# A two-block transformer step on one core: decays one projection chunk later, a modulation slab moved, units in strict turn, a shorter routing chain

## The chip, the cores and the metric

The kernel runs on one core of one Trainium2 chip. The metric is device time in microseconds (us) of one execution, lower is better; times of several executions are given by their median. The engines are named as in the profile: PE (matrix products; PEld its weight loads), DVE (vector), ACT (activation functions), POOL (GpSimd), SP (it only issues transfers here). The 16 DMA engines move all data.

## What is computed

Two transformer blocks, one after the other, on 256 tokens of width 1024, all in 32-bit floats. Cut to what matters:

```python
# first block
h = rmsnorm(x); proj = h @ w_mix_in            # 3592 columns
y_sc  = sc_b * conv(sc_c * sc_h)
g     = -exp(a_log) * softplus(ga + dt_bias)   # decays of the gated delta rule
beta  = sigmoid(gb)
o     = gated_delta_rule_chunked(q, k, v, g, beta)
y_sb  = stick_breaking_attention(sq, sk, sv)
x = x + concat(y_sc, o * silu(gz), y_sb) @ w_mix_out
x = x + (silu(gate) * val) @ w_ffn_down        # gate, val = conv(rmsnorm(x) @ w_ffn_up)
x = rmsnorm(x)
# second block
mod = silu(c) @ w_ada + b_ada                  # six modulation vectors of 1024
h = rms_norm(x) * (1 + sc1) + sh1
x = x + gt1 * rms_norm(attention(h) @ w_out)
h2 = rms_norm(x) * (1 + sc2) + sh2
logits = h2 @ w_router + b_router              # 32 experts, the 4 largest of each token
x = x + gt2 * rms_norm(sum over the 4 experts of gate * expert(h2))
```

## The kernel before

**Weights.** Nearly all the traffic is weights, and SP issues their loads in one fixed order. The dense part reads 67 slabs of 1 MB and 24 slabs of the modulation matrix `w_ada` (1 MB each) into six half slots of pool A. The experts' part reads 32 x 6 slabs of 2 MB (`in_we`, loaded in `load_m`, line 246) into ten slots. `TURNS = "FABADACCEG"` names the pool of each of the ten; slab m goes to the pool of m mod 10, and when the products have read a slab, `free_m` issues the load of the slab ten places on into the slot that came free. The first twelve slabs are those of two fixed experts, so their loads need no routing; the rest are read by numbers that the router gives. The pools are stacked in memory: pools C and G are opened after the dense part has closed its stack `sx`, at the same addresses. C (two slots of 16 KB a partition) lies where the dense part's unit buffers were, G where its normalised tokens were. E's slot holds `hT`, the tokens for the router's logits, until the logits are done.

**Units.** For exactness a dense slab is split into halves ("units"), each a rounded high part (ACT, or POOL; line 407) and the remainder (DVE, or POOL every n-th; line 412). Four buffers of 8 KB hold the units; PE multiplies three times a pair (lines 451, 485 to 487). `unit()` splits up to four units ahead.

**First block.** `weave` (line 124) records several generators in one order: `delta()` (the gated delta rule), `queries()`, `sticks()` (stick-breaking), `silus()`, `projections()` (the filler: 24 matrix products of 256 columns a projection, in chunks of 9, 9 and 6) and `filler()` (two `w_ada` slabs). Each step yields estimates of engine time, and those alone decide who is recorded next; on the chip each engine then works through its own queue in that order. In `delta()` the decays `g` and `beta` come from a few tiny DVE operations (lines 760 to 764); after them PE forms cumulative sums with products of 4 columns (767 to 776), DVE copies them out (`gcol` 771, `grows` 779), PE spreads `grows` over the partitions (785), and from that follow `dec`, `kb`, the products 812, and five levels of 844. `sticks()` goes from products 938/939 over ACT, DVE and POOL to products 962.

**Between the blocks' halves.** After the output projection come a norm and a transposition (line 358) for each of two token halves. While DVE and ACT work on the second half, PE multiplies slabs of `w_ada` with `ada(0)` (line 501, four products of 512 columns a slab): 2 in `filler`, `F0` = 4 between the two transpositions, 1 behind the second, the eighth and the final transposition in passes 0 and 1 of the feed-forward.

```python
            flipped(xn[:, 0, :], 0, take_scaled(lambda kc: col("w_norm_ffn", kc)))
            for _ in range(F0):
                next(fill)
            pool_los["of"] = 1
            split_ahead(1)
            flipped(xn[:, 1, :], 1, take_scaled(lambda kc: col("w_norm_ffn", kc)))
            split_ahead(2)
            pool_los["of"] = 0
            for _ in range(7 - F0 - F00):
                next(fill)
```

Then 11 passes of the feed-forward (`up` twice, `down` twice a pass), the attention of the second block with another `weave`, its output projection (the last `LAST` = 2 units in `last_products`), the routing, and the experts in the order of `ORDER`.

**Routing.** `turned` transposes x, `logits` multiplies it with the router's weights, DVE finds the four largest of each token (`sel`), PE counts places (lines 1579 to 1585), `select` makes a selection matrix `S` (1697), `gather` multiplies it with x (1710), ACT copies the result out (1712), `turn` transposes it (1721), and the first expert's products (1752) begin. `keep_warm` issues products that compute nothing.

Of the kernel before, what the change touches and what calls it, by code (L numbers as in the profile page):

```python
# [11 lines left out]
F32R = mybir.dt.float32r  # L12
BF = mybir.dt.bfloat16
I32 = mybir.dt.int32
AF = mybir.ActivationFunctionType
OP = mybir.AluOpType
# [5 lines left out]
P = 128  # L22
# [6 lines left out]
UW = 1024  # L29
# [7 lines left out]

PLACES = "531240531240531240530125304530412530412530412530412504153045230512340512340521435012345"

TURNS = "FABADACCEG"  # L40
NS = len(TURNS)
F00 = 2
F0 = 4
F1 = 3
LAST = 2

WARM = (4, 6, 9, 1, 2, 9, 12, 20)
# [114 lines left out]
def fl(t):  # L162
    return t.rearrange("p a b -> p (a b)")
# [3 lines left out]
def kernel(ctx: ExitStack, tc: tile.TileContext, x_in, cols_in, rows_in, const_in, cona_in, conb_in, rpb_in,  # L167
                      ws_in, wf_in, we_in, b1_in, b2_in, out, dbg=None):
    nc = tc.nc
# [11 lines left out]

    x = pers.tile([P, 2, D], F32, name="x")
    sx = ctx.enter_context(ExitStack())
    parts = sx.enter_context(tc.tile_pool(name="parts", bufs=4))
    xnp = sx.enter_context(tc.tile_pool(name="xnp", bufs=1))
    hp = sx.enter_context(tc.tile_pool(name="hp", bufs=1))
    cols = hp.tile([P, NKEPT], F32, name="cols")
# [62 lines left out]
    def load_all(names):  # L250
        for m in range(NS):
            if TURNS[m] in names:
                load_m(m)
# [38 lines left out]
    def con(name):  # L292
        a, b = CONST[name]
        return cst[:, a:b]
# [3 lines left out]
    def bank(pool=None):  # L298
        return (pool or ps).tile([P, 512], F32, name="mm")

    def keep_warm(n):

        b = bank()
        for _ in range(n):
            nc.tensor.matmul(b, warm[:, 0:1].to_broadcast([P, P]), warm[:, 0:1].to_broadcast([P, 512]), start=True, stop=True)  # L305

    def rsqrt(r, v, n):

        rsqrt_start(r, v)
        rsqrt_end(r, v, n)  # L310

    def rsqrt_start(r, v):
        nc.scalar.activation(r, v, AF.Ln)  # L313
        nc.scalar.activation(r, r, AF.Exp, scale=-0.5)

    def rsqrt_end(r, v, n):
        a = small.tile([P, 4], F32, name="nwt")
        nc.vector.tensor_mul(a[:, :n], v, r)
        nc.vector.scalar_tensor_tensor(a[:, :n], a[:, :n], -0.5, r, op0=OP.mult, op1=OP.mult)
        nc.vector.scalar_tensor_tensor(r, a[:, :n], 1.5, r, op0=OP.add, op1=OP.mult)  # L320
# [64 lines left out]
    with sx:  # L385
# [11 lines left out]
        def split(u, hi_on=None):  # L397

            s, h = divmod(u, 2)
            s = WS_DENSE[s]  # L400
            raw = s_slab[s][:, h * UW:(h + 1) * UW]
            t = parts.tile([P, 2, UW], F32R, name="u")
            hi, lo = t[:, 0, :], t[:, 1, :]
            if hi_on:
                hi_on.tensor_copy(hi, raw)
            else:
                nc.scalar.activation(hi, raw, AF.Copy)  # L407
            pool_los["n"] += 1
            on_pool = pool_los["of"] and pool_los["n"] % pool_los["of"] == 0
            loads.extend([("A", 0.95), ("G", 2.3) if on_pool else ("V", 1.13)])  # L410
            eng = nc.gpsimd if on_pool else nc.vector
            eng.tensor_tensor(lo, raw, hi, op=OP.subtract)  # L412
            hi_lo[u] = (hi, lo)
            if h == 1:
                slab_read(s)
# [103 lines left out]
        with ExitStack() as s1:  # L519
# [205 lines left out]
            def delta():  # L725
# [36 lines left out]
                    nc.vector.scalar_tensor_tensor(g[:, c, :], ga[:, c, :], -1.0, ea, op0=OP.mult, op1=OP.mult)  # L762
                nc.vector.tensor_scalar(beta, beta, 1.0, None, op0=OP.add)
                nc.vector.reciprocal(beta, beta)
                yield [("v", 1.1)]
                gcp = bank(pg)
                nc.tensor.matmul(gcp[:, 0:4], con("uincl"), g[:, 0, :], start=True, stop=True)
                nc.tensor.matmul(gcp[:, 4:8], ones, g[:, 0, :], start=True, stop=False)
# [231 lines left out]
        with ExitStack() as s2:  # L1000
# [32 lines left out]
            flipped(xn[:, 1, :], 1, take_scaled(lambda kc: col("w_norm_ffn", kc)))  # L1033
            split_ahead(2)
            pool_los["of"] = 0
            for _ in range(7 - F0 - F00):
                next(fill)
            dump("x1", x)
            sf = s2.enter_context(ExitStack())
# [1 line left out]
            with ExitStack() as s3:  # L1041
# [60 lines left out]
                for i in range(NFF // 2):  # L1102
                    up(2 * i)
                    next(biases, None)
                    if i < 2:
                        next(fill)
                    up(2 * i + 1)
                    if i:
                        next(biases, None)
                    if 0 < i < NFF // 2 - 1:  # L1110
                        for j in (2 * i - 2, 2 * i - 1):
                            down(j, (0, 1), *unit())
                    if 2 <= i < 2 + len(WX):
                        n = len(WS) + i - 2
                        s_slab[n] = fx.tile([P, SW], F32, name="w")
                        nc.sync.dma_start(s_slab[n], ws_in[n])
                    if i == 1:
                        for _ in fill:
                            pass
                    if i == 7:  # L1120
                        fill = ada(1)
                    if i >= 7:
                        next(fill)
# [359 lines left out]
            def turned(c, h):  # L1483
                b = bank()
                for k in range(4):
                    nc.tensor.transpose(b[:, k * P:(k + 1) * P], x[:, c, h * 512 + k * P:h * 512 + (k + 1) * P], ident)
                return b
# [14 lines left out]
            b = turned(0, 1)  # L1502
            x_sums(1, 0)
            nc.scalar.activation(fl(hT[:, 1]), b, AF.Copy)
            bs = [turned(1, 0)]
            x_sums(0, 1)
            x_sums(1, 1)
            keep_warm(WARM[4])
            logits(0, 1)
            bs.append(turned(1, 1))  # L1510
            nc.vector.tensor_copy(fl(hT[:, 2]), bs[0])
            v = row_means(ssx)
            rsqrt_start(rx, v)
            nc.scalar.activation(fl(hT[:, 3]), bs[1], AF.Copy)
            rsqrt_end(rx, v, 2)
            for h in range(2):
                logits(1, h)
            dump("x4", x)
            keep_warm(WARM[5])


    for k in "CG":
        pools[k] = ctx.enter_context(tc.tile_pool(name="slabs" + k, bufs=TURNS.count(k), reuse_waits="tile"))
    ek2 = ctx.enter_context(tc.tile_pool(name="ek2", bufs=2, side="right", reuse_waits="tile"))
    psa = ctx.enter_context(tc.tile_pool(name="psm", bufs=1, space=PSUM, reuse_waits="tile"))
# [21 lines left out]
        w.ek = stack.enter_context(tc.tile_pool(name="ek", bufs=2, reuse_waits="tile"))  # L1547
        return w

    load_all("CEG")  # L1550
    s6 = ctx.enter_context(ExitStack())
    w = open_work(s6)

# [25 lines left out]
    nc.tensor.matmul(b[:, 0:NE], con("uincl"), sel[:, 0, :], start=True, stop=True)  # L1579
    nc.tensor.matmul(b[:, NE:2 * NE], ones, sel[:, 0, :], start=True, stop=False)  # L1580
    nc.tensor.matmul(b[:, NE:2 * NE], con("uincl"), sel[:, 1, :], start=False, stop=True)
    nc.tensor.matmul(b[0:NE, 64:96], ones[:, 0:NE], sel[:, 0, :], start=True, stop=False)
    nc.tensor.matmul(b[0:NE, 64:96], ones[:, 0:NE], sel[:, 1, :], start=False, stop=True)
    nc.tensor.matmul(b[0:NE, 96:97], sel[:, 0, :], one_c, start=True, stop=False)
    nc.tensor.matmul(b[0:NE, 96:97], sel[:, 1, :], one_c, start=False, stop=True)
    nc.vector.tensor_tensor(place, b[:, 0:64].rearrange("p (c e) -> p c e", c=2), sel, op=OP.mult)
    cnt = rt.tile([NE, NE + 1], F32, name="cnt")
    nc.scalar.activation(cnt, b[0:NE, 64:97], AF.Copy)
    dump("cnt", cnt)
# [109 lines left out]
                nc.vector.tensor_scalar(slotted(G, c, tb), slot_numbers(tb), pc, gt(c), op0=OP.is_equal, op1=OP.mult)  # L1699
        return tb, S, G  # L1700

    def gather(w, tb, S, G):

        R = P // tb
        n = D // R
        xg = w.ek.tile([P, 512], F32, name="xg")
        b = bank()
        for c in range(2):
            for p in range(R):
                nc.tensor.matmul(b[p * tb:(p + 1) * tb, 0:n], S[:, c, p * tb:(p + 1) * tb],  # L1710
                                 x[:, c, p * n:(p + 1) * n], start=(c == 0), stop=(c == 1))
        nc.scalar.activation(xg[:, 0:n], b[:, 0:n], AF.Copy)
        return R, tb, xg, G

    def turn(w, R, tb, xg, G):
# [112 lines left out]
    def selects(pos):  # L1828
        rank = ORDER[pos]
        pos_, gate_ = by_rank(rank)  # L1830
        return [select(w, first, tb, pos_, gate_ if pos else None) for first, tb in cut(CAPS[rank])]

    blks = [gather(w, *a) for a in selects(0)]
    blks = [turn(w, *a) for a in blks]
    gates()
    chosen = selects(1)
# [301 lines left out]
```

## Time and profile before

| | |
|---|---|
| median of 3 runs | 1470.18 us (1468.39 to 1471.1) |
| the profiled execution's own time | 1470.03 us |
| its span, first to last instruction | 1468.3 us |
| PE busy / DVE / ACT / POOL | 93% / 37% / 31% / 4% |
| bytes moved | 506.66 MB, mean 345 GB/s |
| mean granted PE clock | 0.981 of full |

The profiled execution lies 1.7 us above its span and 0.15 us below the median, so what the rows say is read as if it stood at the median. A busy PE means that matrix products are in flight, not that they run at full rate; PE's granted clock is given as a share, 1.00 for 2.4 GHz and 0.50 for 1.2 GHz. Busy shares are means over stages that have different limits; the time of an edit is read from its own stage.

### The profile page before, as it was taken

What the parts mean: (1) busy time and instruction counts of PE and PEld (TensorE: products, weight loads), DVE (VectorE), ACT (ScalarE), POOL (GpSimd) and SP (SyncE); (2) the same over time, 40 slices, a digit from 0 to 9 for tenths busy, and PEclk for the clock granted to TensorE, in tenths of its full rate; (3) what the DMA queues carried; (4) which work ended last, traced back from release to release, by engine and by line L of the source; (5) the groups of instructions that cost most, each with busy time, mean ns of one, the idle gap of its engine ahead of it and who ended that gap; (6) DMA issues with size and microseconds to landing.
All of it is one profiled execution on the core that took longest, in us unless ns stands there. A gap on an engine that the chain in (4) does not pass through costs nothing.

```text
span 1468.3 us, 21778 instructions
## 1 busy us (share of the span) xinstructions
PE 1358.5 (93%) x8879; PEld 728.9 (50%) x8879; DVE 547.3 (37%) x1259; ACT 453.7 (31%) x972; POOL 55.7 (4%) x32
## 2 busy tenths in 40 slices
PE   8999999999999999999889889899998799899884
PEld 6899789998688753233233223233332233233221
DVE  6754677766757852121121121121211112121112
ACT  6454565554657541111111111111111111111111
POOL 3222010000000000000000000000000000000000
PEclk9999999999999999999999999999999999999997
DMA  7422586656746699999999999999999999999993
GB/s 319 144 87 87 198 327 235 266 212 230 240 172 232 256 384 427 427 428 427 427 428 428 428 428 427 427 427 427 427 427 428 428 427 427 428 427 427 428 428 159
DMA packets 43433, 506.66 MB, mean 345 GB/s; under 512 B 5024, under 2 KB 5280, under 8 KB 6880
## 3 DMA queue, kind: packets, MB, share of 16 engines
q1 hardware_dynamic: 42752, 503.61, 83.3%
q8 instruction: 72, 1.18, 0.3%
q10 hardware_dynamic: 576, 1.61, 0.3%
q14 instruction: 33, 0.27, 0.1%
HBM read 504.14 MB, written 1.05 MB: 344 GB/s over the span
## 4 chain that ended last, share of the span: by engine, by line
PE 56%; DMA 37%; ACT 3%; DVE 3%; issue 1%; SPq 0%; DVEq 0%; ACTq 0%
DMA w<-in_we 37%; PE mm L451 16%; PE mm L1752 13%; PE mm L1795 5%; PE acc L485 3%; PE acc L486 3%; PE acc L487 3%; PE acc L1820 2%; PE mm L1710 2%; PE mm L1790 1%; PE mm L844 1%; PE mm L501 1%; PE acc L1274 1%; PE mm L305 0%; ACT u L407 0%
## 5 line engine op out<-in xcount | busy, mean ns | idle before, releaser
L1752 PE MATMUL mm<-w,xT 128*64 128x512 f32 (+1 forms) x2432 | 434.5, 617 | 52.6 <-DMA w<-in_we 51.7
L1752 PEld LDWEIGHTS mm<-w,xT 128*64 128x64 f32 (+1 forms) x2432 | 129.9, 127 | 341.3 <-issue 257.4
L1761 DVE TENSOR_SCALAR h<-mm 128x256 f32<-128x256 f32 x58 | 24.6, 424 | 685.9 <-PE mm L1757 685.9
L451 PE MATMUL mm<-hT,u 128*128 128x256 f32 x2064 | 265.4, 288 | 0.0
L451 PEld LDWEIGHTS mm<-hT,u 128*128 128x128 f32 x2064 | 254.8, 194 | 13.9 <-issue 10.6
L1762 ACT ACTIVATE a<-h 128x256 f32<-128x256 f32 x58 | 24.2, 417 | 484.3 <-DVE h L1761 484.3
L412 DVE TENSOR_TENSOR u<-w,u 128x1024 fp32r<-128x1024 f32 x115 | 144.6, 1261 | 67.8 <-ACT u L407 64.9
L407 ACT ACTIVATE u<-w 128x1024 fp32r<-128x1024 f32 x133 | 139.0, 1054 | 30.5 <-PE acc L487 23.8
L1795 PE MATMUL mm<-w,aT 128*64 128x512 f32 x640 | 141.9, 595 | 5.5 <-ACT aT L1773 5.4
L1795 PEld LDWEIGHTS mm<-w,aT 128*64 128x64 f32 x640 | 44.3, 137 | 90.2 <-issue 80.0
L1800 ACT ACTIVATE y<-mm 128x512 f32<-128x512 f32 x38 | 22.7, 597 | 208.8 <-PE mm L1795 138.7
L1790 PE MATMUL mm<-w,aT 128*32 128x512 f32 x576 | 65.9, 596 | 10.4 <-ACT aT L1773 9.6
L1710 PE MATMUL mm<-x,S 128*32 128x256 f32 (+1 forms) x448 | 57.7, 465 | 3.5 <-DVE S L1697 3.5
L412 POOL TENSOR_TENSOR u<-w,u 128x1024 fp32r<-128x1024 f32 x19 | 45.8, 2409 | 319.3 <-PE mm L305 203.0
L1083 DVE SCALAR_TENSOR_TENSOR fcv<-mm,cols,fcv 128x255 f32<-128x255 f32 x88 | 42.3, 481 | 24.9 <-ACT fcv L1080 23.4
L1728 ACT ACTIVATE xT<-mm,mod,gs 128x64 f32<-128x64 f32 (+1 forms) x152 | 46.6, 386 | 5.8 <-PE mm L1721 5.2
L1730 DVE TENSOR_SCALAR xT<-mm,gs,mod 128x64 f32<-128x64 f32 (+1 forms) x152 | 38.7, 319 | 14.4 <-PE mm L1721 14.4
L1790 PEld LDWEIGHTS mm<-w,aT 128*32 128x32 f32 x576 | 16.7, 109 | 47.7 <-issue 31.1
L1710 PEld LDWEIGHTS mm<-x,S 128*32 128x32 f32 (+1 forms) x448 | 18.7, 119 | 40.4 <-issue 31.6
L1080 ACT ACTIVATE fcv<-mm,cols 128x256 f32<-128x256 f32 x44 | 20.8, 472 | 55.4 <-PE mm L451 55.4
L1962 POOL TENSOR_TENSOR fs<-fs,x 128x512 f32<-128x512 f32 x1 | 1.3, 1262 | 929.7 <-ACT fr L313 929.7
L485 PE MATMUL acc<-u,gh 128*128 128x512 f32 x88 | 34.9, 397 | 0.0
(555 smaller groups left out, 1368.2 us busy)
## 6 DMA issues: line engine op xcount, KB each, us to landing
w<-in_we SPq DMA_DIRECT2D x192, 2048.0 KB, 34.9
w<-in_ws SPq DMA_DIRECT2D x90, 1024.0 KB, 4.9
nb<-in_rpb SPq DMA_DIRECT2D x4, 512.0 KB, 7.8
w<-in_ws SPq DMA_DIRECT2D x2, 512.0 KB, 6.9
bt<-in_b SPq DMA_DIRECT2D x3, 256.0 KB, 9.8
out<-fs SPq DMA_DIRECT2D x3, 256.0 KB, 2.1
x<-in_x SPq DMA_DIRECT2D x1, 512.0 KB, 4.8
x<-in_x ACTq DMA_DIRECT2D x1, 512.0 KB, 5.0
```

The costliest lines, as they stand in the source:

```text
L407: nc.scalar.activation(hi, raw, AF.Copy)
L412: eng.tensor_tensor(lo, raw, hi, op=OP.subtract)
L451: nc.tensor.matmul(b[:, 0:T], w[:, k, :], h[:, k, :], start=(n == 0), stop=(n == 3 * KC - 1))
L485: nc.tensor.matmul(o, th[:, kc, t], wh[:, w], start=first, stop=False)
L486: nc.tensor.matmul(o, th[:, kc, t], wl[:, w], start=False, stop=False)
L487: nc.tensor.matmul(o, tl[:, kc, t], wh[:, w], start=False, stop=last)
L1083: nc.vector.scalar_tensor_tensor(t[:, sh:], b[:, :T - sh], w(2 - sh), t[:, sh:], op0=OP.mult, op1=OP.add)
L1710: nc.tensor.matmul(b[p * tb:(p + 1) * tb, 0:n], S[:, c, p * tb:(p + 1) * tb], x[:, c, p * n:(p + 1) * n], start=(c == 0), stop=(c == 1))
L1728: nc.scalar.activation(dst, src, AF.Identity, scale=gs[:, kc:kc + 1], bias=mod[:, 24 + kc:25 + kc])
L1752: nc.tensor.matmul(b[p * tb:(p + 1) * tb, :], xT[:, k, q * tb:(q + 1) * tb], w1(p * nr + rd, kc // 4)[:, kc % 4, :], start=(kc == 0), stop ...
L1790: nc.tensor.matmul(b[p * tb:(p + 1) * tb, :], aT[:, 0, j, p0 * tb:(p0 + 1) * tb], w2(bi)[:, j, h * 512:(h + 1) * 512], start=(bi == 0), st ...
L1795: nc.tensor.matmul(b[p * tb:(p + 1) * tb, :], aT[:, rd, j, p0 * tb:(p0 + 1) * tb], w2(bi)[:, j, p * 512:(p + 1) * 512], start=(bi == 0 and ...
```

## The change

The decays' products wait two units longer by the planner's account (`("w", 2.0)`), so that another projection is recorded ahead of them; every order of the first block behind that follows. `F0` goes from 4 to 3, and `ada(0)` ends one pass later. The four unit buffers get names of their own, used strictly in turn. One of the two C slots becomes a pool H, loaded ahead of C. In the routing, one `keep_warm` goes, both transpositions of the second half stand together, their copies both go to DVE, DVE's `place` comes after the first three counting products with the other four in another bank, and the first expert's `gather` is done in two halves of columns, copied by ACT and DVE.

```diff
-TURNS = "FABADACCEG"
+TURNS = "FABADAHCEG"
-F0 = 4
+F0 = 3
...
-    parts = sx.enter_context(tc.tile_pool(name="parts", bufs=4))
+    parts = sx.enter_context(tc.tile_pool(name="parts", bufs=1))
...
-            t = parts.tile([P, 2, UW], F32R, name="u")
+            t = parts.tile([P, 2, UW], F32R, name="u", tag=f"u{u % 4}")
...
                 nc.vector.reciprocal(beta, beta)
-                yield [("v", 1.1)]
+                yield [("v", 1.1), ("w", 2.0)]
                 gcp = bank(pg)
...
-            for _ in range(7 - F0 - F00):
+            for _ in range(6 - F0 - F00):
                 next(fill)
...
                 for i in range(NFF // 2):
                     up(2 * i)
                     next(biases, None)
-                    if i < 2:
+                    if i < 3:
                         next(fill)
...
-                    if i == 1:
+                    if i == 2:
                         for _ in fill:
                             pass
...
-            bs = [turned(1, 0)]
+            bs = [turned(1, h) for h in range(2)]
             x_sums(0, 1)
             x_sums(1, 1)
-            keep_warm(WARM[4])
+            for h in range(2):
+                nc.vector.tensor_copy(fl(hT[:, 2 + h]), bs[h])
             logits(0, 1)
-            bs.append(turned(1, 1))
-            nc.vector.tensor_copy(fl(hT[:, 2]), bs[0])
             v = row_means(ssx)
-            rsqrt_start(rx, v)
-            nc.scalar.activation(fl(hT[:, 3]), bs[1], AF.Copy)
-            rsqrt_end(rx, v, 2)
+            rsqrt(rx, v, 2)
...
-    for k in "CG":
+    for k in "CHG":
...
-    load_all("CEG")
+    load_all("HCEG")
...
+    nc.vector.tensor_tensor(place, b[:, 0:64].rearrange("p (c e) -> p c e", c=2), sel, op=OP.mult)
+    b = bank()
     nc.tensor.matmul(b[0:NE, 64:96], ones[:, 0:NE], sel[:, 0, :], start=True, stop=False)
...
-    nc.vector.tensor_tensor(place, b[:, 0:64].rearrange("p (c e) -> p c e", c=2), sel, op=OP.mult)
...
-    def gather(w, tb, S, G):
+    def gather(w, tb, S, G, m=1):
...
+        for i in range(m):
+            b = bank()
+            o = slice(i * n // m, (i + 1) * n // m)
...
+            if i:
+                nc.vector.tensor_copy(xg[:, o], b[:, 0:n // m])
+            else:
+                nc.scalar.activation(xg[:, o], b[:, 0:n // m], AF.Copy)
...
-    blks = [gather(w, *a) for a in selects(0)]
+    blks = [gather(w, *a, m=2) for a in selects(0)]
```

What this does to the order of instructions is shown at three places. Minus is the kernel before, plus the changed one; `L451` is a projection's products.

PE, first block, around the decays' products (767 to 776) and the spreading of `grows` (785):

```order
 L743 MATMUL mm<-cst,ga_248 128x8 x2
-L451 MATMUL mm<-hT_117,u 128x256 x72
+L451 MATMUL mm<-hT_117,u 128x256 x96
 L767 MATMUL mm<-g,cst 128x4
 L768 MATMUL mm<-g,ones 128x4
...
 L451 MATMUL mm<-hT_117,u 128x256 x15
 L785 MATMUL mm<-grows,cst 128x256 x4
-L451 MATMUL mm<-hT_117,u 128x256 x39
+L451 MATMUL mm<-hT_117,u 128x256 x33
 L803 MATMUL mm<-cst,beta 128x128 x8
-L451 MATMUL mm<-hT_117,u 128x256 x33
+L451 MATMUL mm<-hT_117,u 128x256 x24
```

One projection more (24 products) stands ahead of 767, and 15 fewer between 785 and 812.

DVE at the same place: `gcol` and `grows`, the copies that 785 and `dec` wait for.

```order
 L572 SCALAR_TENSOR_TENSOR qT<-mm,colsm,qT 128x254
 L572 SCALAR_TENSOR_TENSOR qT<-mm,colsm,qT 128x253
+L572 SCALAR_TENSOR_TENSOR vT<-mm,colsm,vT 128x255
+L572 SCALAR_TENSOR_TENSOR vT<-mm,colsm,vT 128x254
+L572 SCALAR_TENSOR_TENSOR vT<-mm,colsm,vT 128x253
+L412 TENSOR_TENSOR u<-w,u 128x1024
 L771 COPY gcol<-mm 128x8
 L779 COPY grows<-mm 4x256
```

Three taps of the added projection's convolution and a unit's remainder now stand ahead of the copies.

PE, between the two transpositions (358) of the second norm, where 501 is the modulation slab's product (x4 is one slab), and on into the feed-forward:

```order
 L358 MATMUL mm<-cst,xn 128x128 x8
-L501 MATMUL mm<-w,silc 32x512 x16
+L501 MATMUL mm<-w,silc 32x512 x12
 L358 MATMUL mm<-cst,xn 128x128 x8
 L501 MATMUL mm<-w,silc 32x512 x4
...
 L501 MATMUL mm<-w,silc 32x512 x4
 L451 MATMUL mm<-hT_117,u 128x256 x96
+L501 MATMUL mm<-w,silc 32x512 x4
+L451 MATMUL mm<-hT_117,u 128x256 x48
```

Three slabs instead of four stand between the transpositions, and the last slab follows the third `up` of the feed-forward.

## Rows read from the trace of the kernel before

**Rows 1.** The page, part 4: the chain that ended last, shares by engine.

```profile
PE 56%; DMA 37%; ACT 3%; DVE 3%; issue 1%; SPq 0%; DVEq 0%; ACTq 0%
```

**Rows 2.** Busy time by stretch: start:end, length, five engines, PEclk, DMA share, GB/s.

```profile
511.00:515.00 4.00, 4.00 (x21) 3.22 (x19) 2.52 (x5) 1.46 (x2) 0.00 (x0) 1.00 0.02 8
515.00:545.00 30.00, 27.80 (x162) 17.95 (x162) 14.86 (x56) 14.33 (x37) 1.36 (x3) 1.00 0.98 397
680.00:1437.00 757.00, 683.46 (x4058) 228.28 (x4054) 140.29 (x454) 115.72 (x318) 0.00 (x0) 0.98 1.01 427
```

**Rows 3.** SP's expert loads: issue (first to last us), then time to landing.

```profile
L246 SPq DMA_DIRECT2D w<-in_we x2: 328/377/426, 514.2 to 514.6; - x2
...
DMA to landing us min/median/max: 7.6/9.9/12.1
...
L246 SPq DMA_DIRECT2D w<-in_we x1: 328/328/328, 523.8 to 523.8; - x1
...
DMA to landing us min/median/max: 9.4/9.4/9.4
...
L246 SPq DMA_DIRECT2D w<-in_we x2: 328/380/433, 533.9 to 534.3; - x2
...
DMA to landing us min/median/max: 9.8/12.5/15.1
```

**Rows 4.** SP's waits, 440 to 640 us: total, times, longest.

```profile
SPq L246 <- DVE s L1304: 20.1, 2, 11.7
...
SPq L246 <- PE acc L487: 9.7, 2, 8.7
```

**Rows 5.** Timeline of SP: the load into the first slot that comes free.

```profile
544.88 0.35 SPq L246 DMA_DIRECT2D w<-in_we  x1
```

**Rows 6.** Timeline of PE, 36 to 60 us: start, us, line, count, [idle before].

```profile
36.44 8.88 PE L451 MATMUL mm<-hT,u 128*128 128x256 f32 x72
47.51 0.39 PE L767 MATMUL mm<-g,cst 128*128 128x4 f32 x2 [2.18 <-DVE g L762]
...
51.01 1.99 PE L785 MATMUL mm<-grows,cst 4*128 4x256 f32 x8
52.92 6.42 PE L451 MATMUL mm<-hT,u 128*128 128x256 f32 x39
```

**Rows 7.** Timeline of DVE at the same place.

```profile
44.94 2.31 DVE L760 SCALAR_TENSOR_TENSOR ga<-ga,gt 128x8 f32<-128x8 f32 x1
...
47.76 1.47 DVE L572 SCALAR_TENSOR_TENSOR qT<-mm,colsm,qT 128x255 f32<-128x255 f32 x3
...
51.98 1.22 DVE L412 TENSOR_TENSOR u<-w,u 128x1024 fp32r<-128x1024 f32 x1
```

**Rows 8.** Two stretches with the lower clock; columns as in rows 2.

```profile
53.50:56.90 3.40, 3.40 (x18) 3.40 (x17) 2.60 (x9) 0.81 (x2) 0.00 (x0) 0.50 0.02 5
...
186.60:190.00 3.40, 3.40 (x18) 2.21 (x11) 2.64 (x4) 2.32 (x3) 2.37 (x1) 0.50 1.07 280
```

**Rows 9.** Timeline of PE at the second norm and the first `up`.

```profile
179.65 3.64 PE L501 MATMUL mm<-w,silc 128*32 128x512 f32 x32
...
186.24 1.62 PE L501 MATMUL mm<-w,silc 128*32 128x512 f32 x8 [1.93 <-DMA w<-in_ws]
187.79 6.99 PE L451 MATMUL mm<-hT,u 128*128 128x256 f32 x48
```

**Rows 10.** Timeline of POOL: the remainder of the feed-forward's first unit.

```profile
184.07 2.35 POOL L412 TENSOR_TENSOR u<-w,u 128x1024 fp32r<-128x1024 f32 x1 [30.29 <-ACT u L407]
```

**Rows 11.** Timeline of PE: where the chains of the first block come back.

```profile
64.92 0.59 PE L812 MATMUL mm<-kb,kT 128*128 128x256 f32 x2
...
95.42 1.15 PE L844 MATMUL mm<-X,LT 64*64 64x64 f32 x32
...
97.04 0.39 PE L939 MATMUL mm<-sqT,skT 64*128 64x128 f32 x4
...
118.79 0.70 PE L962 MATMUL mm<-l,ca 128*128 128x256 f32 x2
```

More of the change, by code (lines that the diff above doesn't have):

```diff
@@ L1706, in gather @@
         xg = w.ek.tile([P, 512], F32, name="xg")
[L1707 to L1712, printed above, removed]
+        for i in range(m):
+            b = bank()
+            o = slice(i * n // m, (i + 1) * n // m)
+            for c in range(2):
+                for p in range(R):
+                    nc.tensor.matmul(b[p * tb:(p + 1) * tb, 0:n // m], S[:, c, p * tb:(p + 1) * tb],
+                                     x[:, c, p * n + o.start:p * n + o.stop], start=(c == 0), stop=(c == 1))
+            if i:
+                nc.vector.tensor_copy(xg[:, o], b[:, 0:n // m])
+            else:
+                nc.scalar.activation(xg[:, o], b[:, 0:n // m], AF.Copy)
         return R, tb, xg, G
```

## The prediction

> **What bounds the kernel now.** I read the page's chain first, then stretches, then single transfers. The chain is shared by PE and DMA [rows 1]: up to the routing the matrix products set the pace, after it the experts' weights do. The stretches say where one hands over to the other. From 680 to 1437 us the DMA engines are full at 427 GB/s while PE waits for them; just ahead, from 511 to 515, they stand nearly still, and from 515 to 545 they move 397 GB/s [rows 2]. So from 515 us on the transfers hardly pause, and the end is that instant plus a fixed amount of bytes. Two things can move the end: everything ahead of 515 us ending earlier, which shifts the whole stream, and bytes that flow where the stream still has gaps. The routing is no such thing by itself: the tenth slab's load, issued second of two at 534.3, lands 15.1 us later at 549.4 [rows 3], and the load into the first slot that comes free is issued at 544.9 [rows 5], 4.5 us before the engines need it.
>
> **The decays' products.** PE stands 2.18 us ahead of line 767 for the decays [rows 6]. The added projection has 24 products; 72 took 8.88 us, 0.123 each [rows 6], so 24 take 2.96 and PE comes to 767 at 36.44 + 8.88 + 2.96 = 48.3, where it was let go at 47.5. The wait goes. What is late next is on DVE. The three taps it was at from 47.76 end at 49.2 [rows 7]; now three taps more (1.47) and a unit's remainder (1.22) [rows 7] stand ahead of the two small copies, for which I take one tap's 0.49 together: `grows` is ready at 52.4. PE went from 767 to 785 in 51.01 - 47.51 = 3.5 us [rows 6] without a wait, so it will be at 785 at 51.8 and wait 0.6. This term: -2.18 + 0.6 = -1.6.
>
> Behind 785 the 39 products took 6.42 us [rows 6] instead of 4.8, because the clock was granted at 0.50 (1.2 GHz) from 53.5 to 56.9 [rows 8]: that costs 1.6. Ahead of this stretch PE had waited (to 47.5), worked, and done the eight products of 785 with four rows each. The stretch does not follow the wait at once, so I leave it where it is: 0, with -1.6 as the other end. The Trainium skill (TensorE: Matmul & The Clock Gate, "Part 1: The HAM clock gate") says that idleness lowers the clock and steady work restores it; by that, closing the wait would return the 1.6 as well. The trace agrees on the two levels, but shows six microseconds between the wait and this drop.
>
> **The modulation slab.** Four slabs take 3.64 us, 0.91 each, between the transpositions, and a fifth waits 1.93 us for its load; the first `up` begins at 187.8 [rows 9]. In the change the slab behind the second transposition is one that PE used without a wait before [rows 9], so this wait goes too. But the `up` then stands at the remainder of its first unit, which POOL finishes at 184.07 + 2.35 = 186.4 [rows 10]. It begins 1.4 us earlier, not 1.9. The product itself is not saved: 0.91 us come back in the feed-forward, which has no idle PE to hide it. Net -0.5. The first `up` took 6.99 us for 48 products instead of 5.9, since the clock was at 0.50 from 186.6 to 190.0 [rows 8]. If the low stretch stays at its place, the earlier start puts 1.4 / 0.246, nearly six, products more into it at twice the time: +0.7, net +0.2. If it goes, 1.1 is gained: net -1.6. I take -0.5, the same loss as before.
> The moved step's queue: on SP each load into a modulation slab's place stands behind its product, now later by an `up` and a slab (48 x 0.123 + 0.91 = 6.8 us), and the loads behind it wait with it. They bring slabs for the next pass, and one pass's four projections alone are 96 x 0.123 = 11.8 us: nothing, as long as SP is ahead by that much.
>
> **H ahead of C.** The two loads issued at 514.2 and 514.6 land by 526.7; the next, issued at 523.8, lands at 533.2 [rows 3], 6.5 us later. A slab of 2.1 MB at 427 GB/s is 4.9 us [rows 2], so 1.6 us of transfer are missing: that load reached an almost empty queue. SP had waited 8.7 us for the last units' products [rows 4]. With strict turns the last two units lie in the buffers 0 and 1, under C; H lies over 2 and 3, whose units are multiplied before, so its load joins the queue while the two ahead are in flight. -1.6. The ends: 0, if the slowness is not the late issue, and the whole shortfall from 515 to 545, 30 x (1 - 397/427) = -2.1 [rows 2]. The gap from 511 to 515 stays: SP's 11.7 us wait there [rows 4] is for D's slot, ahead of H in the queue.
>
> **The routing.** Fewer steps between the last product and the first expert's products free the first slot sooner. The 4.5 us of lead named above hide that; worth 0. If the cover were gone (a drained queue at 545), each microsecond saved there would count.
>
> **The sum.** -1.6 - 0.5 - 1.6 = -3.7 against the profiled execution's 1470.03: 1466.3. That execution is 0.15 below the median, so this is also the forecast of the median.
>
> **Rivals.**
> (1) *The clock rises too.* Both low stretches vanish with the waits ahead of them: 1.6 and 1.1 more, 1463.6. For it: the second stretch begins right after PE's wait. Against it: PE still stands about two microseconds there for the hidden units, and the first stretch comes late. The skill's rule above leads here.
> (2) *Only part arrives.* The late issue was not the reason for the slow transfer (0 for H), and the low clock keeps its place at the `up` (+0.2): -1.6 + 0.2 = -1.4, 1468.6. For it: rows of 397 GB/s show busy engines (0.98), not idle ones. Against it: the queue really was nearly empty at 525.
> (3) *Slower: a chain comes back later than its cover.* The first block's PE order was long enough to hide two chains on DVE, ACT and POOL. From 767 to 812 it took 64.92 - 47.51 = 17.4 us [rows 6, 11]; now the cover is 3.5 + 0.6 + 1.99 + 57 x 0.123 + about 1.5 for line 803 (what is left of 52.92 to 64.92 after 39 and 33 products [rows 6, 11]) = 14.6. From 939 to 962 it took 21.4 us [rows 11]; now 81 projection products and seven groups of 32 at 1.15 [rows 11], 18.0. If the chains need all they had, PE waits 2.8 and 3.4 us, and one more low stretch costs 1.6: -3.7 + 7.8 = +4.1, 1474.1. It is slower by more than 0.2% only from 6.6 of these 7.8. For it: DVE has more ahead of `grows`, and one 8-column operation took 2.31 us beside POOL's work [rows 7]. Against it: part of the 17.4 was the low clock, PE found no wait there before, and DVE's queue holds the later unit's remainder anyway.
>
> **How the numbers follow.** Forecast 0.45, (1) 0.25, (2) 0.24, (3) 0.06. A measurement of this kernel can tell about 0.2%, 2.9 us, from no change, so faster means below 1467.3. All of (1) and some three quarters of the forecast's spread (its ends: H at 0 gives 1467.9, H at -2.1 with the `up` at -1.6 gives 1464.7) lie there: 0.59. Slower takes most of (3): 0.05. The rest, 0.36, is the same. The range from 1463.0 to 1469.4 takes in (1), (2) and the ends of the terms, and leaves out (3) and the tails.
>
> **What would show it.** Right: no wait of PE at 767 and one under a microsecond at 785; the first `up` about 1.4 us earlier against the second transposition; H's load issued some 5 us ahead of C's, with landings 5 us apart from there; the nearly idle stretch before D's load still there, some 2 us earlier. Wrong: waits at 812 or 962; landings still 6 us apart; the stream pausing behind the tenth slab, which would make the routing count after all; a gain above 6 us, which would be the clock.

## The result and the profile after

The changed kernel takes **1481.72 us**, median of 4 (1480.4 to 1483.16), against 1470.41 for the kernel before: a ratio of 1.0077, interval 1.0062 to 1.0091. Forecast were 1466.3 and a range from 1463.0 to 1469.4; it came out slower by 11.3 us, on the side that had 0.05. Its profiled execution took 1482.09 us with a span of 1480.3, 12.0 above the span before.

PE's timeline, first block (start, length, line, what, count, [idle before]). First the changed kernel:

```profile
48.70 0.28 PE L767 MATMUL mm<-g,cst 128*128 128x4 f32 x2
...
52.93 1.99 PE L785 MATMUL mm<-grows,cst 4*128 4x256 f32 x8 [0.79 <-DVE grows L779]
...
65.06 0.59 PE L812 MATMUL mm<-kb,kT 128*128 128x256 f32 x2
...
77.57 1.97 PE L834 MATMUL mm<-cst,Y 64*64 64x64 f32 x32 [3.99 <-DVE Y L828]
...
134.24 1.20 PE L981 MATMUL mm<-z,sv 128*64 128x256 f32 x3 [3.38 <-DVE z L972]
...
169.59 0.50 PE L485 MATMUL acc<-u,yT 128*128 128x512 f32 x1
```

and the first product of the output projection in the kernel before:

```profile
156.78 0.50 PE L485 MATMUL acc<-u,yT 128*128 128x512 f32 x1
```

The wait at 767 [rows 6] is gone and the one at 785 is there with 0.8, as forecast. Then come two that the forecast did not have: 4.0 at 834 for `Y` and 3.4 at 981 for `z`. The block ends 12.8 us later (169.59 against 156.78), so the loss lies here. A low clock stands behind each new wait, in the stretches of the changed kernel (columns as in [rows 2], the granted clock third from the end):

```profile
73.50:75.50 2.00, 0.08 (x1) 0.00 (x0) 2.00 (x1) 0.00 (x0) 2.00 (x1) 1.00 0.00 0
75.50:77.60 2.10, 0.03 (x2) 0.06 (x3) 1.86 (x4) 0.00 (x0) 0.05 (x1) 0.50 0.46 90
...
134.20:139.00 4.80, 4.76 (x20) 3.27 (x22) 1.61 (x3) 0.98 (x2) 0.00 (x0) 0.50 0.45 189
139.00:143.60 4.60, 4.60 (x24) 4.24 (x21) 1.11 (x2) 1.33 (x2) 2.37 (x1) 0.50 0.00 0
```

PE stands still from 73.6; some two microseconds later the granted clock is 0.50 (1.2 GHz), and it stays there to 82.7, five microseconds into the work. Behind 981 nine microseconds of work run at it. Half of the work's time in both is 2.6 + 4.7 = 7.3, which the low clock cost, beside 7.4 of waits.

**What the waits wait for.** DVE's timeline in the changed kernel, then ACT's and POOL's:

```profile
65.91 2.52 DVE L814 TENSOR_TENSOR LT<-mm,dec 128x384 f32<-128x384 f32 x4 [0.46 <-PE mm L813]
71.79 1.23 DVE L412 TENSOR_TENSOR u<-w,u 128x1024 fp32r<-128x1024 f32 x1 [3.36 <-ACT u L407]
72.93 3.77 DVE L826 TENSOR_TENSOR Y<-LT,ca 64x256 f32<-64x256 f32 x4
76.73 0.69 DVE L828 TENSOR_TENSOR Y<-ca,Y 128x512 f32<-128x512 f32 x1
```

```profile
64.53 1.28 ACT L671 ACT_TABLE_LOAD   x1
...
69.13 1.28 ACT L675 ACT_TABLE_LOAD   x1
70.42 0.39 ACT L611 ACTIVATE sqT<-mm 128x256 f32<-128x256 f32 x1
70.70 1.05 ACT L407 ACTIVATE u<-w 128x1024 fp32r<-128x1024 f32 x1
```

```profile
73.06 2.49 POOL L412 TENSOR_TENSOR u<-w,u 128x1024 fp32r<-128x1024 f32 x1 [6.08 <-ACT u L407]
```

`LT` is done at 68.4 and `Y` needs nothing else. But ahead of `Y` in DVE's queue stands the remainder (412) of unit 16, whose rounded part ACT makes only at 70.70, behind two table loads and the activations between them. So DVE stands still for 3.4 us, spends 1.2 on a unit that PE wants only some 20 us later (counted by PE's products, 24 a unit), and then takes 3.8 for the four operations of 826 beside POOL's 73.06 to 75.55. The kernel before had the same wait for ACT, but behind `Y`:

```profile
66.40 1.94 DVE L814 TENSOR_TENSOR LT<-mm,dec 128x384 f32<-128x384 f32 x4
68.38 1.72 DVE L826 TENSOR_TENSOR Y<-LT,ca 64x256 f32<-64x256 f32 x4
70.13 0.69 DVE L828 TENSOR_TENSOR Y<-ca,Y 128x512 f32<-128x512 f32 x1
76.89 1.23 DVE L412 TENSOR_TENSOR u<-w,u 128x1024 fp32r<-128x1024 f32 x1 [6.07 <-ACT u L407]
```

and in its ACT queue the same two table loads stood ahead of the unit's rounded part:

```profile
69.91 1.28 ACT L671 ACT_TABLE_LOAD   x1
...
74.51 1.28 ACT L675 ACT_TABLE_LOAD   x1
75.80 1.06 ACT L407 ACTIVATE u<-w 128x1024 fp32r<-128x1024 f32 x1
```

The second place reads alike. DVE and ACT of the changed kernel:

```profile
130.97 2.52 DVE L412 TENSOR_TENSOR u<-w,u 128x1024 fp32r<-128x1024 f32 x1 [7.88 <-ACT u L407]
133.41 1.28 DVE L972 TENSOR_TENSOR z<-z,ca 128x512 f32<-128x512 f32 x2
```

```profile
123.20 1.57 ACT L969 ACTIVATE z<-z 128x768 f32<-128x768 f32 x2
...
125.26 1.28 ACT L619 ACT_TABLE_LOAD   x1
126.56 1.06 ACT L619 ACTIVATE sz<-sz 128x1024 f32<-128x1024 f32 x1
127.64 1.28 ACT L620 ACT_TABLE_LOAD   x1
128.93 2.00 ACT L407 ACTIVATE u<-w 128x1024 fp32r<-128x1024 f32 x2
```

`z` is ready for 972 at 124.8; the remainder of unit 24, ahead of it, waits until 130.97 for ACT.

**H.** SP's loads in the changed kernel, D, H and the first freed slot:

```profile
L246 SPq DMA_DIRECT2D w<-in_we x1: 328/328/328, 527.8 to 527.8; - x1
...
L246 SPq DMA_DIRECT2D w<-in_we x1: 328/328/328, 532.0 to 532.0; - x1
...
DMA to landing us min/median/max: 13.2/13.2/13.2
...
L246 SPq DMA_DIRECT2D w<-in_we x1: 347/347/347, 557.2 to 557.2; - x1
...
DMA to landing us min/median/max: 9.3/9.3/9.3
```

H goes 6.7 us ahead of C (538.7; forecast were some 5) and lands 5.0 behind the slab before it (540.2), as forecast; C lands at 551.1, still 5.9 behind H. From D's issue at 514.2 [rows 3] to the landing in the first freed slot, issued at 544.9 [rows 5] and landed 9.8 later at 554.7, it was 40.5; it is 527.8 to 566.5, 38.7: 1.8 us less.

**The balance of the spans.** 0.65 up to 743, in a part that is the same in both kernels. From there to 812 28.19 instead of 28.70, with nine products (1.1) more done: -1.6. From 812 to 485 104.53 instead of 91.86, with nine fewer: +13.8. Then 0.6 in the output projection, 0.2 from the norm into the feed-forward (the slab), and -1.6 from there to the end. Sum: 12.0.

### The profile page after: what moved, and what is told of

Its sections match the earlier page's. It is cut to its first block, busy times and chain, and to the rows that moved or that the text cites. A ratio compares the mean times of both kernels' runs of the same rounds, so it can differ in the third digit from the quotient of the medians.

```text
span 1480.3 us, 21789 instructions
## 1 busy us (share of the span) xinstructions
PE 1362.1 (92%) x8881; PEld 735.2 (50%) x8885; DVE 550.3 (37%) x1261; ACT 453.3 (31%) x971; POOL 55.1 (4%) x32
## 3 DMA queue, kind: packets, MB, share of 16 engines
q1 hardware_dynamic: 42752, 503.61, 82.7%
## 4 chain that ended last, share of the span: by engine, by line
PE 52%; DMA 37%; DVE 4%; ACT 4%; issue 1%; SPq 0%; ACTq 0%; DVEq 0%
DMA w<-in_we 36%; PE mm L451 14%; PE mm L1755 13%; PE mm L1798 5%; PE acc L485 2%; PE acc L486 2%; PE acc L487 2%; PE acc L1823 2%; PE mm L1710 2%; PE mm L1793 1%; PE mm L844 1%; ACT u L407 1%; DMA w<-in_ws 1%; DVE u L412 1%; PE acc L1274 1%
## 5 line engine op out<-in xcount | busy, mean ns | idle before, releaser
L451 PE MATMUL mm<-hT,u 128*128 128x256 f32 x2064 | 267.8, 289 | 1.5 <-DVE fcv L1083 0.9
L451 PEld LDWEIGHTS mm<-hT,u 128*128 128x128 f32 x2064 | 256.1, 194 | 16.9 <-issue 11.0
L1710 PE MATMUL mm<-x,S 128*32 128x256 f32 (+2 forms) x456 | 56.7, 455 | 3.2 <-DVE S L1695 3.2
```

What stands on the lines that cost most here:

```text
L451: nc.tensor.matmul(b[:, 0:T], w[:, k, :], h[:, k, :], start=(n == 0), stop=(n == 3 * KC - 1))
L1710: nc.tensor.matmul(b[p * tb:(p + 1) * tb, 0:n // m], S[:, c, p * tb:(p + 1) * tb], x[:, c, p * n + o.start:p * n + o.stop], start=(c == 0) ...
```

## The experiments

Theory Q: DVE's queue, as read above. Rivals: O, another part of the change loses the time; C, the chains simply have less cover. Medians of 4 to 12 runs, and the ratio to the kernel before with its interval, timed on the same chip. e1 to e4, e5 to e8 and e9 to e12 ran on three different chips, where the kernel before had medians of 1471.0, 1470.4 and 1471.0; a difference of less than a microsecond between runs of two groups therefore says little. In kernels with inserted lines the line numbers are up to 16 higher.

| run | median, us | ratio to before |
|---|---|---|
| e1_no_w | 1470.00 | 0.9991 (0.9979 to 1.0003) |
| e2_w_alone | 1481.42 | 1.0073 (1.0057 to 1.0089) |
| e3_held | 1472.88 | 1.0015 (1.0004 to 1.0027) |
| e4_fill | 1475.66 | 1.0030 (1.0019 to 1.0040) |
| e5_behind_bv | 1468.91 | 0.9986 (0.9973 to 1.0000) |
| e6_w3 | 1486.48 | 1.0107 (1.0082 to 1.0133) |
| e7_fill767 | 1468.42 | 0.9985 (0.9974 to 0.9997) |
| e8_late16 | 1475.00 | 1.0027 (1.0013 to 1.0040) |
| e9_fill_start | 1467.30 | 0.9971 (0.9958 to 0.9984) |
| e10_before_fill | 1469.68 | 0.9985 (0.9974 to 0.9997) |
| e11_no_turn | 1470.22 | 0.9987 (0.9975 to 1.0000) |
| e12_no_ada | 1467.45 | 0.9976 (0.9962 to 0.9990) |

**Which part of the change.** e1_no_w takes the planner's wait out of the changed kernel, e2_w_alone puts it alone into the kernel before.

```diff
-                yield [("v", 1.1), ("w", 2.0)]
+                yield [("v", 1.1)]
```

> The changed kernel without the two units that the decays' products wait longer: the first block's order is that of before, all other parts of the change stay. Theory Q (DVE's queue): all of the loss comes from the first block's new order, where a unit's remainder that waits for ACT stands ahead of Y and of z on DVE. Then PE's waits at 834 (4.0) and 981 (3.4) are gone, the 2.2 at 767 is back, and the time is that of before less what the other parts give: 1468.3 (1470.4 - 0.5 - 1.6), between 1466.5 and 1470. Rival O (one of the other parts loses the time): 1481 to 1484.

> The kernel before with nothing but the two units' wait added. Theory Q: the whole loss is here, and the other parts' gain is not: 1481.7 + 0.5 + 1.6 = 1483.8, between 1481.5 and 1485.5, with PE's waits at 834 and 981 (4.0 and 3.4) and the granted clock at 0.50 behind each. Rival O: 1468.8 (1470.4 - 1.6, the term of the decays' products).

1470.0 and 1481.4: the whole loss hangs on this one line; O falls. In e2 PE waits the same 4.0 and 3.4. e2 came out 0.1 below what was expected and 0.3 below the changed kernel, so between these two medians the other parts show none of the 2.1 that was claimed for them, and e1 lies at the upper end of its range (more below).

**Is it the remainder in DVE's queue?** e3_held records the same queues, except that the remainders of units 16 and 24 are kept back and issued behind 828 and behind 972; e8_late16 does so for unit 16 alone; e5_behind_bv for both, with unit 24 behind 890. The diff is that of e3; `let_go` issues what was kept back, a second one stands behind 972, in e5 behind the `bv` of 890 instead, and e8 has 16 alone in `LATE`.

```diff
+LATE = (16, 24)
...
-            eng.tensor_tensor(lo, raw, hi, op=OP.subtract)
+            def rest():
+                eng.tensor_tensor(lo, raw, hi, op=OP.subtract)
...
+            if u in LATE:
+                behind.append(rest)
+            else:
+                rest()
...
                 nc.vector.tensor_sub(Y, cona("id64")[:, None, :].to_broadcast([P, 8, 64]), Y)
+                let_go()
```

> The changed kernel; every queue is recorded as it is, but on DVE the remainders of units 16 and 24 are issued behind Y (828) and behind z (972), instead of ahead of them. Theory Q: Y no longer stands behind the 3.4 us for which DVE waited for ACT, and z not behind the 7.9; the waits at 834 and 981 are under 1 us together, and the two new stretches at 0.50 go with them: 7.4 of waits, 2.6 (half of 77.6 to 82.7) and 4.7 (half of 134.2 to 143.6), so 1481.7 - 14.7 = 1467.0, between 1465.5 and 1469.5. Rival C (the chains simply have less cover in the new order, rival 3 of the prediction): only the remainders' own 1.2 and 2.5 come off, the clock stays low behind what is left: 1477 to 1479.

1472.9, between what Q and C expected, and both waits are gone (0.6 is left at 981, for ACT's `sv`). So C falls: the chains do have cover. But it is 5.9 us above the 1467.0. The wait of DVE for ACT was still in the queue, and it met the next operation behind: in this kernel's waits of PE, and DVE's timeline,

```profile
PE mm L909 <- DVE bv L905: 1.9, 1, 1.9
```

```profile
124.33 2.54 DVE L421 TENSOR_TENSOR u<-w,u 128x1024 fp32r<-128x1024 f32 x1 [4.88 <-ACT u L414]
126.90 0.69 DVE L905 TENSOR_TENSOR bv<-bv,mm 64x512 f32<-64x512 f32 x1
```

(905 and 909 are lines 890 and 894 of the changed kernel, 421 is 412). That cost 1.9 and a stretch at 0.50 from 129.6 to 132.8.

> As the run before with units 16 and 24 issued later on DVE, but unit 24's remainder one step later still: behind the `bv` of line 890, for which PE had waited 1.9 us there. Theory Q (DVE's queue): with no waiting remainder ahead of any operation that PE waits for, that wait goes and with it the half clock from 129.6 to 132.6 (1.5): 1472.9 - 1.9 - 1.5 = 1469.5, between 1468 and 1471. Rival C (the chains have less cover in the new order): PE waits at 890's reader for the chain itself, 1472 to 1474.

1468.9, with no wait there any more: 12.8 us below the changed kernel by the places of two instructions in one queue. It is still 1.9 above the 1467.0 that e3 was to reach and 2.6 above the forecast; where that lies is told with the prediction's terms.

> The changed kernel with unit 16's remainder alone issued behind Y on DVE. Theory Q, each of the two places by itself: the wait at 834 (4.0) and its low clock (2.6) go, the one at 981 (3.4, with 4.7 of clock) stays: 1475.1, between 1473.5 and 1477. If the second wait depends on the first (what the first no longer holds up is waited for at 981): 1478 to 1481.

1475.0: the first place alone is worth 6.7 of the 6.6 expected, and the second does not depend on it.

**How much of it is the clock?** e4_fill leaves DVE and ACT as they are and lets PE do empty products in both waits (17 here, 14 ahead of 981).

```diff
                 b = bank(pg)
+                idle(b, 17)
```

> The changed kernel with products that compute nothing in front of 834 (17) and of 981 (14), on PE, so that it works through most of both waits; DVE and ACT as they are. If the low clock follows from PE standing still there: 0.50 no longer granted behind either wait, 2.6 + 4.7 = 7.3 come back, 1474.4 (1473 to 1476), and the waits themselves stay paid. If the low clock has another cause: still 0.50 behind both, 1481.7 (1481 to 1483.5).

1475.7, and in its stretches the clock is full:

```profile
73.50:84.00 10.50, 10.33 (x106) 6.81 (x105) 4.95 (x6) 4.25 (x6) 2.14 (x1) 1.00 0.28 100
128.60:144.00 15.40, 15.17 (x109) 11.51 (x109) 7.88 (x9) 4.85 (x9) 4.01 (x2) 1.00 0.39 137
```

6.1 us came back with both waits still paid: the 7.4 us in which PE stood still cost nearly twice that. The Trainium skill (TensorE: Matmul & The Clock Gate, "Part 1: The HAM clock gate") has idleness lower the clock. The runs agree: 0.50 behind both waits with PE standing still, 1.00 with the same waits filled.

**A dose of the same thing.** e6_w3 asks the planner for three units instead of two.

```diff
-                yield [("v", 1.1), ("w", 2.0)]
+                yield [("v", 1.1), ("w", 3.0)]
```

> The changed kernel with three units of waiting for the decays' products instead of two. By the order of the queues Y on DVE then stands ahead of the next unit's remainder again, as before the change; z still stands behind one. Theory Q: no wait at 834 and no low clock there, the wait at 981 with its 10 us of low clock stays: 1481.7 - 4.0 - 2.6 = 1475.1, between 1473.5 and 1477. Rival C (less cover, the more the later the decays' products come): the wait at 834 grows, 1483 or more.

1486.5 (the profiled one of its four runs took 1481.5, the others 1486.5 to 1487.4). The expectation of Q was wrong: the wait at 981 stayed, as it had said, but the one at 834 did not go, and two came on top. I had read that no remainder stands between 814 and 826 any more, and not that it now stands ahead of 814, where it waits 7.5 us for ACT. The wait at 785 has another source: a remainder ahead of `grows` took 3.31 us, beside a remainder of POOL's from 50.8 to 53.2, instead of 1.22. Waits of PE and DVE's timeline in this kernel:

```profile
PE mm L981 <- DVE z L972: 3.4, 1, 3.4
PE mm L785 <- DVE grows L779: 3.2, 1, 3.2
PE mm L834 <- DVE Y L828: 2.3, 1, 2.3
PE mm L690 <- DVE LT L814: 1.6, 1, 1.6
```

```profile
50.93 3.31 DVE L412 TENSOR_TENSOR u<-w,u 128x1024 fp32r<-128x1024 f32 x1
...
76.96 1.23 DVE L412 TENSOR_TENSOR u<-w,u 128x1024 fp32r<-128x1024 f32 x1 [7.49 <-ACT u L407]
78.10 1.95 DVE L814 TENSOR_TENSOR LT<-mm,dec 128x384 f32<-128x384 f32 x4
```

By time alone this run cannot tell Q from C, which had said 1483 or more; e3, e5 and e8 do.

**The old wait, filled.** e7_fill767 has before's order of the first block, and 9 empty products where PE stood ahead of 767; e10_before_fill is the kernel before with nothing else. e11_no_turn and e12_no_ada are e7 without H and the strict turn, and without the slab's move; their further edits are the second and the third diff, against the changed kernel.

```diff
                 gcp = bank(pg)
+                idle(gcp, 9)
```

```diff
-TURNS = "FABADAHCEG"
+TURNS = "FABADACCEG"
...
-    parts = sx.enter_context(tc.tile_pool(name="parts", bufs=1))
+    parts = sx.enter_context(tc.tile_pool(name="parts", bufs=4))
```

```diff
-F0 = 3
+F0 = 4
...
-                    if i < 3:
+                    if i < 2:
                         next(fill)
```

> The changed kernel without the two units' wait (1470.0), with 9 products that compute nothing ahead of 767: they took 0.23 each in the run that filled 834 and 981, so 2.1 of the 2.2 us for which PE stands there; DVE and ACT as they are. If the low clock behind 767 follows from PE standing still: no 0.50 between 48 and 63 (13.8 us of it in that kernel's profiled execution, 3.4 in that of the kernel before), so 1.7 to 6 us less: 1464 to 1468.3, say 1467. If it doesn't: 1470 (1469 to 1471), with a stretch at 0.50 still there.

1468.4, 0.1 above the first range. The wait is gone but for 0.2, and with it the long stretch directly behind it; but a stretch at 0.50 is still there, as it is in the kernel before [rows 8] and in the changed one, which has no wait at 767 either. The stretches of e1, of e7 and of the changed kernel:

```profile
48.76:62.60 13.84, 13.84 (x56) 11.63 (x56) 7.44 (x18) 2.33 (x4) 0.00 (x0) 0.52 0.20 77
```

```profile
53.90:57.40 3.50, 3.50 (x19) 3.50 (x18) 2.89 (x9) 1.38 (x2) 0.00 (x0) 0.51 0.02 5
```

```profile
54.80:57.80 3.00, 3.00 (x15) 2.95 (x15) 2.10 (x7) 0.00 (x0) 0.15 (x1) 0.54 0.54 169
```

So the short stretch from about 54 does not follow from the wait at 767. The 12 runs of e7 lie between 1467.1 and 1468.9, while those of the kernel before spread from 1467.6 to 1475.9 on the same chip. That spread is told below.

> The kernel before with nothing but the 9 empty products ahead of 767. Against the same fill with the other three parts of the change in place (1468.4), what is missing here is the slab, H and the routing together. By the rows of the traces so far (H 1.8 on the transfers from D's issue to the first freed slot, the slab's move -0.2) that is 1.6: 1470.0. By the prediction's terms (0.5 + 1.6 + 0) it is 2.1: 1470.5. If none of them arrives: 1468.4.

> The filled kernel (767 with 9 empty products, the other three parts in place: 1468.4) with H and the strict turn of the units undone. If the late load of C was the 1.6 to 1.8 us of transfer that the rows show: 1470.1 (1469.5 to 1470.8). If the stream makes it up later, by running nearer to its full rate behind the routing: 1468.4.

> The filled kernel (1468.4) with the modulation slab back between the transpositions. The prediction's term (-0.5 for the move): 1468.9. By the rows of the changed kernel (first `up` sooner by 2.6 us, but then short waits of 0.6, 0.6 and 0.9 and the slab's own 0.9: +0.2 in all): 1468.2. If the half clock at the first `up` stays away here as it did in the kernel with nothing but the two units' wait, where that stage was 1.7 shorter than before: 1466.6.

Timed side by side: 1469.7, 1470.2 and 1467.5. The intervals against the kernel before overlap. Compared directly (an estimate, by drawing anew from the 12 runs of each), e12 is below e11 by 2.8, interval 1.4 to 4.0, and below e10 by 2.2, interval 0.2 to 3.1. From D's issue to the first freed slot's landing: e7 39.2, e12 38.9 with H, e10 41.0, e11 40.3 without. By these rows H is worth 1.1 to 2.1, and the times of e12 give no sign that the stream makes it up later. By time alone H is not separated: e12 differs from e11 also by the slab's move, and from e10 also by the routing. That the slab's move pays is not shown either: only e7 and e12 differ by it alone, on two chips, 1468.4 with it and 1467.5 without. From the first transposition to the end of the second pass e12's profiled execution is 2.0 shorter than e7's, both with the full clock at the first `up`: e7 begins the `up` 2.0 sooner and loses 4.0 behind it, with the slab's own 1.0, 0.6 of waiting for POOL and 1.3 for the convolution among them. The routing was not tried by itself.

**The start.** e9_fill_start is e7 with 14 empty products more in the three waits ahead of the first transpositions.

```diff
-                    flipped_half(xn[:, c, :], c, h, take)
+                    flipped_half(xn[:, c, :], c, h, take, (4, 0, 2, 8)[2 * h + c])
```

> The filled kernel (1468.4) with 14 more empty products in the three waits of PE ahead of the first transpositions (1.0, 0.5 and 1.9 us). If the half clock from 13 to 17 us follows from these waits: it goes, and 1.3 to 2 us with it (half of 13.3 to 16.8): 1466.7 (1466 to 1467.3). If it has another cause: 1468.4 to 1469, the stretch still there.

1467.3, the lowest of the runs and faster than before by its interval. The time lies at the end of the first range, but by luck, since the mechanism did not come: in its profiled execution the half clock begins at 10.7 all the same and lasts seven microseconds, and the last eight empty products took 3.6 us instead of the 1.8 that they take at the full clock:

```profile
13.61 3.62 PE L309 MATMUL mm<-warm 128*128 128x512 bf16 x8
```

In that execution, alone among the profiled ones, the stretch from about 54 to 57 is absent. Why the median fell stays open: that execution (1469.0) is one of the slowest of its 12.

## Why the prediction was wrong

- **The decays' products, up to 812: right.** No wait at 767, 0.8 at 785 (forecast 0.6), and -1.6 up to 812, net of the products that moved (forecast -1.6). Leaving the low stretch from 53.5 to 56.9 in its place was right too: it stands in the changed kernel from about 54.8 to 57.8, without a wait at 767, so the half of rival 1 that let it go with that wait is refuted.
- **The step that failed** is that this term ended at 785. "What is late next is on DVE" was followed to `grows` and no further, while the order of all four engines changes to the end of the block. The part from 812 on, left out of the sum at nothing, measured +13.8.
- **Rival 3** had the kind of thing, a chain that comes back later than PE's cover, but at 812 and 962 and with 0.06. It compared PE's cover before and after, and asked whether the chains are long. They are not: e5 ends the same chains in time. What mattered was which instruction stands ahead of theirs in DVE's queue and what that one waits for. "DVE's queue holds the later unit's remainder anyway" was put down against the rival and was the very cause: before, it was held behind `Y`, now ahead of it. The trace of before had the numbers: the remainder's wait of 6.07 for ACT, and ACT's two table loads, with the work between them, from 69.9 to 75.8 in front of it.
- **The clock** was priced in rival 3 at one stretch of 1.6. Two came, of 7 and 10 us, worth 7.3 by the rows, and 6.1 came back in e4.
- **The modulation slab:** forecast -0.5, bounds +0.2 to -1.6. The wait of 1.9 went [rows 9], and the `up` began 2.8 us behind the second transposition instead of 4.6, so 1.8 sooner (forecast 1.4; 2.6 sooner if counted from the first transposition, between which and the second one slab less stands). But PE then waited 0.6 for `hT`, 0.6 for POOL and 0.9 for the feed-forward's convolution, and the slab's 1.0 came back in the feed-forward: +0.2 between the profiled executions. Rival 1's clock did rise there, and the gain was given back all the same.
- **H: right.** -1.8 on the transfers, -1.6 by the balance of the spans (forecast -1.6). **Routing:** 0, as forecast, so far as the rows show.
- **What is left of the forecast.** With DVE's queue put right (e5) the profiled execution is 1.5 shorter from 743 to 485 than before, and 1.6 shorter in the transfers, as forecast. Against that it loses 0.7 in the output projection and 0.6 at the slab's move, and 0.9 ahead of 743, in a part that is the same in both kernels. So even without the failed step the forecast of 1466.3 was too low; of the 0.7, PE waited 0.4 for a unit's remainder on DVE, and the rest stays open.

## What to carry to other kernels

Where a planner's number reorders in-order queues, go down each queue to the end of the reordered stretch, and for every instruction that came to stand ahead of a chain ask what that instruction itself waits for; its wait becomes the chain's. Work that nobody needs soon (a unit split four ahead) belongs behind the chain's operations on its engine. And a wait of PE of three or four microseconds is to be priced with the low clock behind it: behind the waits of 4.0 and 3.4 it cost about as much again, while behind waits of about 2 it came in some executions and not in others (next section).

## What was not expected of the hardware

**The same wait, with the low clock or without it.** e10 and e12 both wait some 1.9 us for the slab's load, at the same place. PE's timeline, then the stretch behind, of e10:

```profile
186.42 1.74 PE L505 MATMUL mm<-w,silc 128*32 128x512 f32 x8 [1.97 <-DMA w<-in_ws]
```

```profile
186.40:190.50 4.10, 4.08 (x20) 2.57 (x21) 3.33 (x5) 2.66 (x3) 2.55 (x2) 0.58 1.07 282
```

and of e12:

```profile
186.47 1.06 PE L505 MATMUL mm<-w,silc 128*32 128x512 f32 x8 [1.87 <-DMA w<-in_ws]
```

```profile
186.40:190.50 4.10, 4.03 (x33) 3.19 (x34) 3.33 (x6) 2.81 (x3) 2.72 (x2) 1.00 1.07 296
```

20 products in one, 33 in the other. The wait of 2.2 at 767 likewise: in the profiled execution of e1 the clock fell directly behind it, for nearly 14 us; in that of the kernel before, with the same order of PE there, it stayed at 1.00 for six microseconds behind it, and the stretch that then came [rows 8] stands also in kernels without this wait (above). What starts that one stays open; in the kernel before, in e7 and in the changed kernel alike PE had just done the eight products of 785, with four rows each. The spread of the kernel before most likely comes from the wait at 767: nothing but its fill (e10) left 3.5 us, 1466.7 to 1470.2, where the kernel before had 8.4 on the same chip, and with the other parts in place it left 1.9 in e7 where e1 had 5.6.

**DVE beside POOL.** The four operations of 826 took 1.72 alone (before, and e8) and 3.77 beside POOL's remainder of 2.49. The Trainium skill (SBUF — State Buffer, "SBUF: two separate sides") says that the two engines share a pair of ports which one of them holds for a whole instruction while the other stands still; against a POOL operation that reads SBUF, this holds for DVE operations with two inputs there. The operations of 826 have two such inputs, and the 2.05 more, of 2.49, agrees with it, as do the 2.09 more of the remainder ahead of `grows` in e6. By the rows, the wait at 834 was longer by about 2 for it: the late `Y` met POOL's remainder, which the earlier `Y` of before and of e8 did not.
